# Kept weight units, an in-place residual and a split first tile between the output projection and the MLP

## The chip, the cores and the metric

The kernel runs as one program on one core of a Trainium2 chip. A core has a matrix engine (TensorE, PE in the profile, with its weight loads in a row of their own, PEld), a vector engine (VectorE, DVE), a scalar engine (ScalarE, ACT), GpSimd (POOL) and SyncE (SP), whose queue starts most of the transfers here. Each engine works through its own queue in order, and waits for the others by semaphores. The metric is the device time of the whole program in microseconds; smaller is better.

## The reference

One layer of a hybrid trunk for 384 tokens (256 of a prompt, 8 times 16 of running streams) of width 2048. The part that matters here is how the mixer's result becomes the input of the MLP:

```python
def rmsnorm(x, g):
    xf = x.astype(jnp.float32)
    y = xf * lax.rsqrt(jnp.mean(xf * xf, axis=-1, keepdims=True) + EPS)
    return (y * g.astype(jnp.float32)).astype(x.dtype)
...
    merged = (gates[:, :, 0] * br_pool + gates[:, :, 1] * br_ssd).astype(u.dtype)
    out = merged @ p['w_out']
...
    x = x + rmsnorm(m, p['g_mix_post'])
    hdn = jnp.square(jax.nn.relu(rmsnorm(x, p['g_mlp_pre']) @ p['w_up'])) @ p['w_down']
    x = x + rmsnorm(hdn, p['g_mlp_post'])
```

`w_out` is 2048 by 2048, `w_up` 2048 by 8192, `w_down` 8192 by 2048, all float32.

## The kernel before

The 384 tokens are three blocks of 128, called b = 0, 1, 2. Every large product is made with operands split into a high and a low part of type float32r, so that one product takes three matmuls: high by high, high by low, low by high (`mm3`, lines 80 to 83, and `mm` in `moving`, lines 644 to 646). The input that is split on the chip is split by two instructions: ACT copies it to the high part, DVE subtracts that from the original and writes the low part.

A weight unit is 128 by 1024 numbers, 512 KB. `wfetch` loads it into a tile `w`, `wsplit` writes its parts `wh` (ACT, line 72) and `wl` (DVE, line 74). Each of the three tiles has three buffers, so a unit's transfer waits until the unit three before it has been split, and a unit's split waits until PE has used the unit three before it for the last time.

The output projection is computed by `moving`: tokens are the stationary operand, the weights move, 512 columns at a time. There are four column groups (nb = 0 to 3) of eight units each, and three PSUM tiles `wo`, one for each block. For nb = 0 to 2 every unit is used for the three blocks at once. For nb = 3 the last three units are kept (`tail` = 3): they are used first for block 0, then for block 1, then for block 2, so that block 0 is complete earlier. After each block `done(b)` runs: ACT squares the result and sums it (line 692), for nb = 3 `postnorm` computes the root of the mean in a chain of small instructions on DVE and one on ACT (lines 663 to 674), and DVE multiplies the result with the norm's weight into the tile `hm` (line 695). When all three blocks are through, the residual is formed: `x1 = hm * y + x1` for each block and each 512 columns (line 707 on DVE; two of the twelve by line 704 on ACT and 705 on POOL). `x1` holds the input tokens until then; they are loaded by three transfers of 1 MB.

Next `x1` is transposed for the MLP: for each of 16 groups of 128 channels (k) PE transposes the three blocks into one PSUM tile `trm` (line 717), ACT writes the high part `x1h` (line 721) and DVE the low part `x1l` (line 722), 384 columns each. Four PSUM tiles `ss` serve these transposes and later the tile `bc`, so the transposes of group k wait until `x1l` of group k - 4 is written. The MLP's first product, tile `up0` (line 751 to 754), takes 48 matmuls of 384 columns over these 16 groups; `up1` and the others follow (line 756).

In the meantime the second norm is computed: ACT squares `x1` in twelve pieces (line 733), `postnorm` makes a factor for each token, DVE puts it on a diagonal (`dg`, line 737), and PE spreads it over the partitions with one float32 matmul with a matrix of ones (`bc`, line 739). ACT copies the result to `r2`, which the first evacuation of an up tile needs (line 759).

A scheduler of the language decides where in an engine's queue each instruction stands; the queue is then fixed. `issue_after` (in `wsplit`, through the variable `hold`) forces the split of the second half of `up0`'s weights and of those of `up1` behind the residual's instructions:

```python
        gate = [root[0], None]
...
            if i == 0:
                gate[1] = ins
...
                    hold[:] = gate
                    half(ps, 1, wload(io["w_up"][0, 1], "up0_1"), xs2)
```

Of the kernel before, what the change touches and what calls it, by code (L numbers as in the profile page):

```python
# [14 lines left out]
P = 128  # L15
T = 384
# [3 lines left out]
DM = 2048  # L20
KD = DM // P
# [13 lines left out]
def build(ctx, tc, io):  # L35
    nc = tc.nc
    v, s, te, gp, sy = nc.vector, nc.scalar, nc.tensor, nc.gpsimd, nc.sync
# [19 lines left out]
    hold = [None, None]  # L57

    def behind(ins):
        return nullcontext() if ins is None else tc.issue_after(ins.ins)  # L60

    def wfetch(src, name):
        w = wpool.tile([P, 1024], F32, tag="w", name=f"w_{name}")
        sy.dma_start(w, src)
        return w, name

    def wsplit(f):
        w, name = f
        h = wpool.tile([P, 1024], F32R, tag="wh", name=f"wh_{name}")
        l = wpool.tile([P, 1024], F32R, tag="wl", name=f"wl_{name}")  # L70
        with behind(hold[0]):
            s.activation(h, w, AF.Copy)  # L72
        with behind(hold[1]):
            v.tensor_tensor(l, w, h.bitcast(F32), ALU.subtract)  # L74
        return h, l

    def wload(src, name):
        return wsplit(wfetch(src, name))

    def mm3(out, wh, wl, xh, xl, first, last):  # L80
        te.matmul(out, wh, xh, start=first, stop=False)  # L81
        te.matmul(out, wh, xl, start=False, stop=False)  # L82
# [550 lines left out]

    x1 = res.tile([P, 3, DM], F32, name="x1")
    r2 = res.tile([P, T], F32, name="r2")

    def moving(o, units, lhs, tail, done):
        nk = len(lhs)

        def mm(b, wh, wl, k, k2):  # L640
            t = slice(b * P, b * P + P)
            c = slice(k2 * 512, k2 * 512 + 512)
            mh, ml = lhs[k][0][:, t], lhs[k][1][:, t]
            te.matmul(o[b], mh, wh[:, c], start=k == 0, stop=False)  # L644
            te.matmul(o[b], mh, wl[:, c], start=False, stop=False)  # L645
            te.matmul(o[b], ml, wh[:, c], start=False, stop=k == nk - 1)  # L646

        n = len(units)
        for kp in range(n - tail):
            wh, wl = wload(*units[kp])  # L650
            for k2 in range(2):
                for b in range(3):
                    mm(b, wh, wl, kp * 2 + k2, k2)
        w = [wload(*units[kp]) for kp in range(n - tail, n)]
        for b in range(3):
            for i, (wh, wl) in enumerate(w):
                for k2 in range(2):
                    mm(b, wh, wl, (n - tail + i) * 2 + k2, k2)
            done(b)

    root = [None]

    def postnorm(pool, st, b, name):
        pre, ms, rt, y = (pool.tile([P, 1], F32, tag=f"n{i}", name=f"n{i}_{name}{b}", bufs=3) for i in range(4))
        v.tensor_tensor(pre, st[:, b, 0:1], st[:, b, 1:2], ALU.add)
        v.tensor_tensor(pre, pre, st[:, b, 2:3], ALU.add)
        v.tensor_scalar(pre, pre, 1.0 / DM, EPS, ALU.mult, ALU.add)
        root[0] = s.activation(rt, st[:, b, 3:4], AF.Sqrt, bias=pre, scale=1.0 / DM)
# [4 lines left out]
        v.tensor_tensor(y, y, ms, ALU.mult)  # L673
        return y

    blk = lambda i: slice(i * 512, i * 512 + 512)
    for b in range(3):
        sy.dma_start(x1[:, b, :], io["x_tok"][b])
    with tc.tile_pool(name="phf", bufs=1, side="right", reuse_waits="tile") as pf, tc.tile_pool(
        name="phf2", bufs=2, side="right", reuse_waits="tile"  # L680
    ) as pf2:
        hm = pf.tile([P, 3, DM], F32, name="hm")
        st = pf.tile([P, 3, 4], F32, name="st1")
        ys = []
        for nb in range(4):
            gpo = pf2.tile([P, 512], F32, tag="gpo", name=f"gpo{nb}")
            sy.dma_start(gpo, io["g_mix_post"][blk(nb)].partition_broadcast(P))
            o = [mmtile(f"wo{nb}_{b}") for b in range(3)]

            def done(b):  # L690
                q = pf2.tile([P, 512], F32, tag="q", name=f"q1_{nb}_{b}")
                s.activation(q, o[b], AF.Square, accum_out=st[:, b, nb : nb + 1])
# [4 lines left out]
            moving(o, [(io["w_out"][nb, kp], f"wo{nb}_{kp}") for kp in range(8)], ms_, 3 if nb == 3 else 0, done)  # L697
        gate = [root[0], None]
        for i in range(4):
            for b in range(3):  # L700
                xb = x1[:, b, blk(i)]
                if b == 1 and i >= 2:
                    hb = hm[:, b, blk(i)]
                    s.activation(hb, hb, AF.Copy, scale=ys[b])
                    gp.tensor_tensor(xb, xb, hb, ALU.add)
                    continue
                ins = v.scalar_tensor_tensor(
                    out=xb, in0=hm[:, b, blk(i)], scalar=ys[b], in1=xb, op0=ALU.mult, op1=ALU.add
                )
            if i == 0:  # L710
                gate[1] = ins
    pga = ctx.enter_context(tc.tile_pool(name="pga", bufs=1, reuse_waits="tile"))
    xs2 = []
    for k in range(KD):
        tr = sstile(f"trm{k}")
        for b in range(3):
            te.transpose(tr[:, b * P : b * P + P], x1[:, b, k * P : k * P + P], ident)
        h = pga.tile([P, T], F32R, name=f"x1h{k}")
        l = pga.tile([P, T], F32R, name=f"x1l{k}")
        g1 = vec[:, V_GMLP + k : V_GMLP + k + 1]  # L720
        s.activation(h, tr[:, :T], AF.Copy, scale=g1)  # L721
        v.scalar_tensor_tensor(out=l, in0=tr[:, :T], scalar=g1, in1=h.bitcast(F32), op0=ALU.mult, op1=ALU.subtract)
        xs2.append((h, l))
    mpool.close()

    with tc.tile_pool(name="phg", bufs=1, reuse_waits="tile") as pg, tc.tile_pool(
# [3 lines left out]
        for b in range(3):  # L730
            for i in range(4):
                q = pg2.tile([P, 512], F32, tag="q3", name=f"q2_{b}_{i}")
                s.activation(q, x1[:, b, blk(i)], AF.Square, accum_out=st[:, b, i : i + 1])
        dg = pg.tile([P, 3, P], F32, name="dg2")
        for b in range(3):
            y = postnorm(pg2, st, b, "n2")
            v.tensor_scalar(dg[:, b, :], ident, y, None, ALU.mult)
        bc = sstile("bc2")
        te.matmul(bc[:, :T], ones, dg.rearrange("p b t -> p (b t)"), start=True, stop=True)
# [6 lines left out]
        for c8 in range(NC):  # L746
            hh = []
            for f8 in range(8):
                f = c8 * 8 + f8
                if f == 0:  # L750
                    ps = mmtile("pj_up0")[:, :T]
                    half(ps, 0, wload(io["w_up"][0, 0], "up0_0"), xs2)
                    hold[:] = gate
                    half(ps, 1, wload(io["w_up"][0, 1], "up0_1"), xs2)
                else:
                    ps = proj([io["w_up"][f, 0], io["w_up"][f, 1]], xs2, f"up{f}")
                    hold[:] = [None, None]
# [158 lines left out]
```

## Time and profile before

| What | Time |
|---|---|
| median of three runs | 2858.26 us (2857.53 to 2859.85) |
| the profiled execution, its time | 2857.06 us |
| the profiled execution, its span | 2855.3 us |
| PE busy | 99% of the span |
| DVE, ACT, POOL busy | 55%, 38%, 4% of the span |
| mean granted PE clock | 0.997 |

The span is the time from the first to the last recorded instruction; the execution's own time is 1.76 us more. A row of the timeline gives the start, the duration, the engine, the line of the source, the operation, what is written and read, the shape and how many like it were merged; in brackets stands how long the engine had been idle before it and who ended that. The durations of matmuls are modelled and overlap; the distance from one start to the next is what a matmul costs in a sequence.

### The profile page before, as it was taken

The page shows a single profiled execution, that of the slowest core. Times are in us where ns is not written, and L with a number is a line of the kernel's source. Part 1 is how long each engine was busy: PE and PEld are TensorE (multiplying, and loading weights), DVE is VectorE, ACT ScalarE, POOL GpSimd, SP SyncE. Part 2 cuts the span into 40 slices and gives each one's busy share as a digit, 9 for nine tenths or more (in the row PEclk, how much of TensorE's full clock was granted, in tenths as well). Part 3 has the DMA queues.
Part 4 walks back from the last instruction along what each step waited for, and adds up shares of the span by engine and source line. Part 5 has one row for each costly group of instructions (what it writes and reads, how often), then busy time and mean ns, then how long its engine had stood idle before and what let it go on. Part 6 is the DMA issues. An engine that isn't in the chain of part 4 may idle for free.

```text
span 2855.3 us, 39378 instructions
## 1 busy us (share of the span) xinstructions
PE 2830.0 (99%) x15855; PEld 2678.6 (94%) x15855; DVE 1568.3 (55%) x2231; ACT 1084.8 (38%) x1560; POOL 115.3 (4%) x163
## 2 busy tenths in 40 slices
PE   9999999999999999999999999999999999999998
PEld 8999999999999999999999987989899998989896
DVE  7674335678778778777533334524444444444445
ACT  5343224345345345444422234433233333323233
POOL 0000000001001001011000000000000000000001
PEclk9999999999999999999999999999999999999999
DMA  6444445466456566466644453344444344333343
GB/s 204 138 132 142 137 140 193 144 211 218 159 203 216 161 205 212 162 213 234 203 153 148 144 189 119 126 133 126 126 128 129 126 129 130 126 129 130 126 127 117
DMA packets 141656, 448.78 MB, mean 157 GB/s; under 512 B 17201, under 2 KB 40817, under 8 KB 136865
## 3 DMA queue, kind: packets, MB, share of 16 engines
q1 hardware_dynamic: 133152, 410.14, 44.7%
q0 software_dynamic: 8320, 36.13, 3.3%
q8 instruction: 124, 2.03, 0.3%
q14 instruction: 60, 0.48, 0.1%
HBM read 404.48 MB, written 41.72 MB: 156 GB/s over the span
## 4 chain that ended last, share of the span: by engine, by line
PE 95%; DVE 2%; ACT 1%; issue 1%; DMA 0%; SPq 0%; DVEq 0%; ACTq 0%
PE pj_up L82 6%; PE pj_up L83 6%; PE pj_up L81 6%; PE wd L645 6%; PE wd L646 6%; PE wd L644 6%; PE pj_x L83 5%; PE pj_x L81 5%; PE pj_x L82 5%; PE pj_sp L83 3%; PE pj_z L81 3%; PE pj_sp L82 3%; PE pj_z L82 3%; PE pj_sp L81 3%; PE pj_z L83 3%; PE pj_gb L81 2%
## 5 line engine op out<-in xcount | busy, mean ns | idle before, releaser
L82 PE MATMUL pj_up<-x1l,wh_up 128*128 128x384 f32 x1024 | 343.2, 335 | 0.0
L81 PE MATMUL pj_up<-x1h,wh_up 128*128 128x384 f32 x1024 | 343.0, 335 | 0.0
L83 PE MATMUL pj_up<-x1h,wl_up 128*128 128x384 f32 x1024 | 342.7, 335 | 0.0
L74 DVE TENSOR_TENSOR wl_wd<-w_wd,wh_wd 128x1024 fp32r<-128x1024 f32 x128 | 156.9, 1226 | 263.1 <-ACT wh_wd L72 263.1
L646 PE MATMUL wd<-wh_wd,hl 128*128 128x512 f32 x768 | 298.9, 389 | 0.0
L645 PE MATMUL wd<-wl_wd,hh 128*128 128x512 f32 x768 | 298.9, 389 | 0.0
L644 PE MATMUL wd<-wh_wd,hh 128*128 128x512 f32 x768 | 298.7, 389 | 0.0
L72 ACT ACTIVATE wh_wd<-w_wd 128x1024 fp32r<-128x1024 f32 x128 | 135.9, 1062 | 351.0 <-PE wd L646 284.4
L74 DVE TENSOR_TENSOR wl_up<-w_up,wh_up 128x1024 fp32r<-128x1024 f32 x128 | 156.9, 1226 | 198.0 <-ACT wh_up L72 198.0
L72 ACT ACTIVATE wh_up<-w_up 128x1024 fp32r<-128x1024 f32 x128 | 135.8, 1062 | 325.8 <-PE pj_up L82 265.1
L81 PE MATMUL pj_x<-xgh,wh_x 128*128 128x384 f32 x768 | 258.2, 336 | 0.0
L82 PE MATMUL pj_x<-xgl,wh_x 128*128 128x384 f32 x768 | 257.8, 336 | 0.0
L83 PE MATMUL pj_x<-xgh,wl_x 128*128 128x384 f32 x768 | 257.7, 336 | 0.0
L81 PEld LDWEIGHTS pj_up<-x1h,wh_up 128*128 128x128 f32 x1024 | 192.5, 188 | 0.7 <-ACT x1h L721 0.4
L82 PEld LDWEIGHTS pj_up<-x1l,wh_up 128*128 128x128 f32 x1024 | 192.6, 188 | 0.4
L83 PEld LDWEIGHTS pj_up<-x1h,wl_up 128*128 128x128 f32 x1024 | 192.4, 188 | 0.1
L644 PEld LDWEIGHTS wd<-wh_wd,hh 128*128 128x128 f32 x768 | 144.2, 188 | 29.9
L646 PEld LDWEIGHTS wd<-wh_wd,hl 128*128 128x128 f32 x768 | 144.1, 188 | 29.9
L645 PEld LDWEIGHTS wd<-wl_wd,hh 128*128 128x128 f32 x768 | 144.1, 188 | 29.8
L83 PE MATMUL pj_z<-xgh,wl_z 128*128 128x384 f32 x512 | 171.0, 334 | 0.0
L81 PE MATMUL pj_z<-xgh,wh_z 128*128 128x384 f32 x512 | 171.0, 334 | 0.0
L82 PE MATMUL pj_z<-xgl,wh_z 128*128 128x384 f32 x512 | 171.0, 334 | 0.0
(279 smaller groups left out, 6145.6 us busy)
## 6 DMA issues: line engine op xcount, KB each, us to landing
w_up<-w_up SPq DMA_DIRECT2D x128, 512.0 KB, 3.4
w_wd<-w_down SPq DMA_DIRECT2D x128, 512.0 KB, 3.4
w_x<-w_in SPq DMA_DIRECT2D x96, 512.0 KB, 4.3
w_z<-w_in SPq DMA_DIRECT2D x64, 512.0 KB, 4.4
w_sp<-w_ssd SPq DMA_DIRECT2D x64, 512.0 KB, 3.5
w_ga<-w_in SPq DMA_DIRECT2D x32, 512.0 KB, 3.4
w_pp<-w_pp SPq DMA_DIRECT2D x32, 512.0 KB, 3.4
hs<-ssm SPq DMA_DIRECT2D x16, 1024.0 KB, 5.6
```

What stands on the lines that cost most here:

```text
L72: s.activation(h, w, AF.Copy)
L74: v.tensor_tensor(l, w, h.bitcast(F32), ALU.subtract)
L81: te.matmul(out, wh, xh, start=first, stop=False)
L82: te.matmul(out, wh, xl, start=False, stop=False)
L83: return te.matmul(out, wl, xh, start=False, stop=last)
L644: te.matmul(o[b], mh, wh[:, c], start=k == 0, stop=False)
L645: te.matmul(o[b], mh, wl[:, c], start=False, stop=False)
L646: te.matmul(o[b], ml, wh[:, c], start=False, stop=k == nk - 1)
```

## The change

Between the output projection and the up projection four things are different.

1. For nb = 3 five units are kept instead of three. The split parts of the first three live in the usual buffers; those of the last two have tiles of their own (`eh`, `el`). Each block thus has 30 matmuls in a row instead of 18.
2. `hm` is gone. `x1` takes the product of the projection and the norm's weight, and the residual is formed in place right after each block's root: `x1 = x1 * y + xt`. The input tokens come in twelve tiles `xt` of 256 KB with six buffers. All twelve residual instructions are on DVE; the two on ACT and the two on POOL are gone, as is the forced order (`hold`, `gate`).
3. The transposes are made for blocks 0 and 1 first (256 columns in one PSUM tile), then for block 2 (128 columns). Tile `up0` is computed in two parts as well: 48 matmuls of 256 columns over blocks 0 and 1, then 48 of 128 columns for block 2. Its two weight units stay until both parts are done.
4. The diagonal of the second norm is split into a high and a low part, and `bc` is made by two float32r matmuls instead of one float32 matmul.

```diff
-        with behind(hold[0]):
-            s.activation(h, w, AF.Copy)
-        with behind(hold[1]):
-            v.tensor_tensor(l, w, h.bitcast(F32), ALU.subtract)
+        s.activation(h, w, AF.Copy)
+        v.tensor_tensor(l, w, h.bitcast(F32), ALU.subtract)
...
-        w = [wload(*units[kp]) for kp in range(n - tail, n)]
+        w = [wload(*units[kp]) for kp in range(n - tail, n - max(0, tail - 3))]
+        for kp in range(n - max(0, tail - 3), n):
+            f, name = wfetch(*units[kp])
+            h = pool.tile([P, 1024], F32R, name=f"eh_{name}")
+            l = pool.tile([P, 1024], F32R, name=f"el_{name}")
+            s.activation(h, f, AF.Copy)
+            v.tensor_tensor(l, f, h.bitcast(F32), ALU.subtract)
+            w.append((h, l))
...
-    for b in range(3):
-        sy.dma_start(x1[:, b, :], io["x_tok"][b])
...
+            if nb == 3:
+                for b in range(3):
+                    for i in range(4):
+                        xt[b, i] = pf2.tile([P, 512], F32, tag="xt", name=f"xt{b}_{i}", bufs=6)
+                        sy.dma_start(xt[b, i], io["x_tok"][b][:, blk(i)])
...
                 s.activation(q, o[b], AF.Square, accum_out=st[:, b, nb : nb + 1])
+                v.tensor_tensor(x1[:, b, blk(nb)], o[b], gpo, ALU.mult)
                 if nb == 3:
-                    ys.append(postnorm(pf2, st, b, "n1"))
-                v.tensor_tensor(hm[:, b, blk(nb)], o[b], gpo, ALU.mult)
...
-        gate = [root[0], None]
-        for i in range(4):
-            for b in range(3):
-                xb = x1[:, b, blk(i)]
-                if b == 1 and i >= 2:
-                    hb = hm[:, b, blk(i)]
-                    s.activation(hb, hb, AF.Copy, scale=ys[b])
-                    gp.tensor_tensor(xb, xb, hb, ALU.add)
-                    continue
-                ins = v.scalar_tensor_tensor(
-                    out=xb, in0=hm[:, b, blk(i)], scalar=ys[b], in1=xb, op0=ALU.mult, op1=ALU.add
-                )
+                    y = postnorm(pf2, st, b, "n1")
+                    for i in range(4):
+                        xb = x1[:, b, blk(i)]
+                        v.scalar_tensor_tensor(out=xb, in0=xb, scalar=y, in1=xt[b, i], op0=ALU.mult, op1=ALU.add)
+            moving(
+                o, [(io["w_out"][nb, kp], f"wo{nb}_{kp}") for kp in range(8)], ms_, 5 if nb == 3 else 0, done, pf
+            )
...
+    def turn(k, b0, b1):
+        tr = sstile(f"trm{k}_{b0}")
+        n = (b1 - b0) * P
+        for b in range(b0, b1):
+            te.transpose(tr[:, (b - b0) * P : (b - b0 + 1) * P], x1[:, b, k * P : k * P + P], ident)
+        h, l = (x[:, b0 * P : b1 * P] for x in xs2[k])
+        g1 = vec[:, V_GMLP + k : V_GMLP + k + 1]
+        s.activation(h, tr[:, :n], AF.Copy, scale=g1)
+        v.scalar_tensor_tensor(out=l, in0=tr[:, :n], scalar=g1, in1=h.bitcast(F32), op0=ALU.mult, op1=ALU.subtract)
+
+    w0 = [wload(io["w_up"][0, q], f"up0_{q}") for q in range(2)]
+    up0 = mmtile("pj_up0")[:, :T]
+
+    def up_first(b0, b1):
+        t = slice(b0 * P, b1 * P)
+        for k in range(KD):
+            h, l = w0[k // 8]
+            c = slice(k % 8 * P, k % 8 * P + P)
+            mm3(up0[:, t], h[:, c], l[:, c], xs2[k][0][:, t], xs2[k][1][:, t], k == 0, k == KD - 1)
+
     for k in range(KD):
-        tr = sstile(f"trm{k}")
...
+        turn(k, 0, 2)
+    up_first(0, 2)
+    for k in range(KD):
+        turn(k, 2, 3)
+    up_first(2, 3)
...
-        dg = pg.tile([P, 3, P], F32, name="dg2")
+        dg = pg.tile([P, 2, 3, P], F32R, name="dg2")
         for b in range(3):
             y = postnorm(pg2, st, b, "n2")
-            v.tensor_scalar(dg[:, b, :], ident, y, None, ALU.mult)
+            v.tensor_scalar(dg[:, 0, b], ident, y, None, ALU.mult)
+            v.scalar_tensor_tensor(
+                out=dg[:, 1, b], in0=ident, scalar=y, in1=dg[:, 0, b].bitcast(F32), op0=ALU.mult, op1=ALU.subtract
+            )
         bc = sstile("bc2")
-        te.matmul(bc[:, :T], ones, dg.rearrange("p b t -> p (b t)"), start=True, stop=True)
+        for i in range(2):
+            te.matmul(bc[:, :T], onesr, dg[:, i].rearrange("p b t -> p (b t)"), start=i == 0, stop=i == 1)
```

More of the change, by code (lines that the diff above doesn't have):

```diff
@@ L635, in build, with moving @@
     r2 = res.tile([P, T], F32, name="r2")
-    def moving(o, units, lhs, tail, done):
+    blk = lambda i: slice(i * 512, i * 512 + 512)
+    def moving(o, units, lhs, tail, done, pool=None):
         nk = len(lhs)
@@ L659, in moving @@
             done(b)
-    root = [None]
     def postnorm(pool, st, b, name):
@@ L676, in build @@
     blk = lambda i: slice(i * 512, i * 512 + 512)
-    for b in range(3):
-        sy.dma_start(x1[:, b, :], io["x_tok"][b])
+    pga = ctx.enter_context(tc.tile_pool(name="pga", bufs=1, reuse_waits="tile"))
     with tc.tile_pool(name="phf", bufs=1, side="right", reuse_waits="tile") as pf, tc.tile_pool(
@@ L681, in build @@
     ) as pf2:
-        hm = pf.tile([P, 3, DM], F32, name="hm")
         st = pf.tile([P, 3, 4], F32, name="st1")
-        ys = []
+        xt = {}
         for nb in range(4):
@@ L692, in done @@
                 s.activation(q, o[b], AF.Square, accum_out=st[:, b, nb : nb + 1])
+                v.tensor_tensor(x1[:, b, blk(nb)], o[b], gpo, ALU.mult)
                 if nb == 3:
-                    ys.append(postnorm(pf2, st, b, "n1"))
-                v.tensor_tensor(hm[:, b, blk(nb)], o[b], gpo, ALU.mult)
-            moving(o, [(io["w_out"][nb, kp], f"wo{nb}_{kp}") for kp in range(8)], ms_, 3 if nb == 3 else 0, done)
-        gate = [root[0], None]
-        for i in range(4):
-            for b in range(3):
-                xb = x1[:, b, blk(i)]
-                if b == 1 and i >= 2:
-                    hb = hm[:, b, blk(i)]
-                    s.activation(hb, hb, AF.Copy, scale=ys[b])
-                    gp.tensor_tensor(xb, xb, hb, ALU.add)
-                    continue
-                ins = v.scalar_tensor_tensor(
-                    out=xb, in0=hm[:, b, blk(i)], scalar=ys[b], in1=xb, op0=ALU.mult, op1=ALU.add
-                )
-            if i == 0:
-                gate[1] = ins
@@ L712, in build @@
-    pga = ctx.enter_context(tc.tile_pool(name="pga", bufs=1, reuse_waits="tile"))
-    xs2 = []
-    for k in range(KD):
-        tr = sstile(f"trm{k}")
[L716 to L723, printed above, removed]
+                    y = postnorm(pf2, st, b, "n1")
@@ new lines, in done @@
+                    for i in range(4):
[4 more added lines that the diff above has]
+            )
+    xs2 = [
+        (pga.tile([P, T], F32R, name=f"x1h{k}"), pga.tile([P, T], F32R, name=f"x1l{k}")) for k in range(KD)
+    ]
+    def turn(k, b0, b1):
[7 more added lines that the diff above has]
+        v.scalar_tensor_tensor(out=l, in0=tr[:, :n], scalar=g1, in1=h.bitcast(F32), op0=ALU.mult, op1=ALU.subtract)
@@ L750, in build @@
                 if f == 0:
[L751 to L754, printed above, removed]
+                    ps = up0
                 else:
                     ps = proj([io["w_up"][f, 0], io["w_up"][f, 1]], xs2, f"up{f}")
-                    hold[:] = [None, None]
                 t = pg2.tile([P, T], F32, tag="t", name=f"ht{f}")
```

3 lines of the change are left out of this document (1 added, 2 removed).

## The prediction

> **What bounds the kernel now.** I read the page first, then the matmuls of the stage in order of time, then the same stretch by windows, and last what ACT and DVE did in it.
>
> ```profile
> span 2855.3 us, 39378 instructions
> PE 2830.0 (99%) x15855; PEld 2678.6 (94%) x15855; DVE 1568.3 (55%) x2231; ACT 1084.8 (38%) x1560; POOL 115.3 (4%) x163
> ```
>
> PE sets the time, so only places where PE waits or runs slowly can give anything. The stage in question is one:
>
> ```profile
> 1772.01 0.39 PE L646 MATMUL wo<-wh_wo,ml 128*128 128x512 f32 x1
> 1773.31 0.66 PE L717 MATMUL trm<-cst,x 128*128 128x128 f32 x4 [0.47 <-DVE x L707]
> 1777.17 1.12 PE L717 MATMUL trm<-cst,x 128*128 128x128 f32 x4 [3.21 <-DVE x L707]
> 1793.60 0.33 PE L82 MATMUL pj_up<-x1l,wh_up 128*128 128x384 f32 x1
> 1798.49 0.88 PE L739 MATMUL bc<-dg,cst 128*128 128x384 f32 x2
> 1799.56 0.34 PE L81 MATMUL pj_up<-x1h,wh_up 128*128 128x384 f32 x1
> 1802.68 0.33 PE L81 MATMUL pj_up<-x1h,wh_up 128*128 128x384 f32 x1
> ...
> 1772.20:1776.60 4.40, 1.29 (x9) 0.77 (x7) 4.22 (x11) 3.99 (x7) 2.48 (x2) 0.98 0.42 121
> 1776.60:1783.40 6.80, 5.84 (x23) 4.68 (x23) 5.84 (x10) 4.81 (x12) 0.56 (x1) 0.51 0.37 145
> 1783.40:1793.70 10.30, 10.30 (x70) 10.10 (x69) 8.98 (x23) 10.30 (x31) 0.00 (x0) 1.00 0.23 66
> ```
>
> The projection ends at 1772.24, `up0` at 1793.60, tile `up2` begins at 1802.68; after that PE runs without a gap, so the start of `up2` is my mark. PE waits 3.2 us for block 2's residual, and for 6.8 us it has half its clock (0.51; the columns behind the five engines are granted clock, DMA share and GB/s). In the third window ACT is busy all the time: it feeds the transposes' high parts and the second norm's squares. From 1772.24 to 1802.68 are 30.44 us. At the steps worked out below, 96 matmuls of 384 columns (16.6), 48 transposes (4.0), a dozen changes between the two (1.0) and `bc` (0.9) are 22.5 us; the other 7.9 are waits and half clock, and no change here can give more than these.
>
> **The change part by part.** *Kept units.* The same matmuls run in another order: no PE time. Units 6 and 7 have tiles of their own; only unit 5's split waits for a buffer, as here:
>
> ```profile
> 1752.04 1.06 ACT L72 ACTIVATE wh_wo<-w_wo 128x1024 fp32r<-128x1024 f32 x1 [3.02 <-PE wo L646]
> 1753.13 1.23 DVE L74 TENSOR_TENSOR wl_wo<-w_wo,wh_wo 128x1024 fp32r<-128x1024 f32 x1 [2.85 <-ACT wh_wo L72]
> w_up<-w_up SPq DMA_DIRECT2D x128, 512.0 KB, 3.4
> ```
>
> The tail of 90 matmuls (0.227 us from start to start) now begins at 1751.8; unit 5 is ready at 1754.36 and needed 12 matmuls in, at 1754.6: just in time. Unit 7's buffer is free at about 1750.3 and its split done 3.4 + 1.06 + 1.23 us later, 1756.1, needed at 1757.3. Cost 0, and the lateness itself if a transfer is late. Block 0's result then comes at 1758.6, block 1's at 1765.4, so their residuals end near 1765 and 1770 under block 1's and 2's matmuls. The two waits for `x1` of 0.5 and 3.2 us are gone. On SP's queue six `xt` transfers now stand ahead of `up1`'s second unit and wait for DVE's residuals; they are issued by 1769, and that unit is needed after 1794. Cost 0.
>
> *In front of block 2's residual.* In the changed queue of DVE three weight splits (`up0` twice, `up1` once) stand ahead of block 2's product; the forced order that held two of them back is gone. They start when block 1's residuals are done, about 1770.05.
>
> ```profile
> 1774.44 1.99 ACT L72 ACTIVATE wh_up<-w_up 128x1024 fp32r<-128x1024 f32 x2
> 1790.84 1.22 DVE L74 TENSOR_TENSOR wl_up<-w_up,wh_up 128x1024 fp32r<-128x1024 f32 x1
> 1772.44 0.60 ACT L692 ACTIVATE q<-wo 128x512 f32<-128x512 f32 x1 [1.66 <-PE wo L646]
> 1776.37 2.74 DVE L707 SCALAR_TENSOR_TENSOR x<-hm,n_n,x 128x512 f32<-128x512 f32 x4
> 1775.24 1.09 DVE L673 TENSOR_TENSOR n_n<-n_n,n_n 128x1 f32<-128x1 f32 x1
> 1777.68 2.00 ACT L721 ACTIVATE x1h<-trm,vec 128x384 fp32r<-128x384 f32 x4 [1.26 <-PE trm L717]
> 1779.02 2.18 DVE L722 SCALAR_TENSOR_TENSOR x1l<-trm,vec,x1h 128x384 fp32r<-128x384 f32 x4
> ```
>
> A merged row of n gives the step from one to the next: (2.74 - 0.75) / 3 = 0.665 for a residual of 512 columns, (2.18 - 0.61) / 3 = 0.52 for `x1l` of 384, hence 0.39 for 256 and 0.26 for 128; likewise on ACT 0.47 for `x1h`, 0.93 for 1024 columns, hence 0.37 for 256 and 0.28 for 128. A weight split steps by 1.14. The three splits end at 1773.47, block 2's product at 1774.13, and the first `x1l` at 1774.8. (The 1.09 us of one 1-column instruction while POOL ran its two additions goes away with them; it lay in the wait of 3.2 us.)
>
> *First part of `up0`.* The work is 32 transposes, 48 matmuls of 256 columns, and a penalty where a matmul follows transposes:
>
> ```profile
> 566.26 1.12 PE L581 MATMUL su<-xst,bst 128*128 128x256 f32 x8
> 1786.00 0.49 PE L717 MATMUL trm<-cst,x 128*128 128x128 f32 x3
> 1786.25 0.42 PE L81 MATMUL pj_up<-x1h,wh_up 128*128 128x384 f32 x1
> 1786.51 0.49 PE L717 MATMUL trm<-cst,x 128*128 128x128 f32 x3
> 1792.04 0.33 PE L81 MATMUL pj_up<-x1h,wh_up 128*128 128x384 f32 x1
> 1792.21 0.33 PE L82 MATMUL pj_up<-x1l,wh_up 128*128 128x384 f32 x1
> ```
>
> Three transposes take 0.25 (0.083 each), a matmul behind them 0.26 instead of 0.173, so 0.087 a change; a float32r matmul of 256 columns (1.12 - 0.28) / 7 = 0.12. Sum 2.7 + 5.8 + 13 x 0.087 = 9.6 us. The waits: 0.7 for the first `x1h` (behind block 2's square on ACT, so 1772.44 + 0.6 + 0.5 against 1772.9, when the four groups that have buffers are transposed), 1.1 for the first `x1l` (it frees the transposes' buffer), and then block 2's four residuals: in DVE's queue they stand between `x1l` of groups 3 and 4, 1776.3 to 1778.9, and PE, which needs `x1l` of group 4 to go on, stops from 1777.3 to 1779.45, 2.1 us. Together 3.9; the part ends at 1772.24 + 9.6 + 3.9 = 1785.7.
>
> *Second part.* Four transposes and a first `x1h` of 128 columns: PE goes on at 1786.7 and is through the first matmul and one of `up1` by 1787.1. Left are 12 transposes (1.0), 12 changes (1.04) and 47 matmuls of 128 columns. No row of this trace has float32r at 128 columns. The nearest rows:
>
> ```profile
> 551.82 1.06 PE L542 MATMUL pp<-Bk,xdw 128*128 128x128 f32 x8
> L542 PE MATMUL pp<-Bk,xdw 128*128 128x128 f32 x128 | 16.9, 275 | 0.0
> L581 PE MATMUL su<-xst,bst 128*128 128x256 f32 x128 | 17.9, 282 | 0.0
> ```
>
> Low end: 0.12 for 256 columns and 0.173 for 384 on a line give 0.067 for 128. High end: the plain float32 product of just this shape, two records of (1.06 - 0.275) / 7 = 0.112, so 0.224. I take 0.224, the row that has the shape; the split into two parts pays three loads of the same weights either way, and one third of the columns. Then `up0` ends at 1787.1 + 2.04 + 47 x 0.224 = 1799.7. In a sentence apart: the Trainium skill, "TensorE: Matmul & The Clock Gate", section on the back-to-back issue gap, gives about 81 ns for each pair of weight load and matmul at 128 columns; by it this part would end at 1793.0, 6.7 us earlier (no run shows it yet; the transposes' 0.083 agrees). That would not gain 6.7 us, for the reason that follows.
>
> *`bc` and what is queued behind it.* In the changed PE queue `bc` stands directly behind `up0`, and 47 of the 48 matmuls of `up1` stand behind `bc`. In the old queue `bc` came 28 matmuls later, under which the second norm was hidden. When is `bc`'s input ready?
>
> ```profile
> 1791.83 0.66 ACT L733 ACTIVATE q<-x 128x512 f32<-128x512 f32 x1
> 1792.44 0.66 ACT L733 ACTIVATE q<-x 128x512 f32<-128x512 f32 x1
> 1793.67 0.68 ACT L668 ACTIVATE n_n<-st,n_n 128x1 f32<-128x1 f32 x3
> L737 DVE TENSOR_SCALAR dg<-cst,n_n 128x128 f32<-128x128 f32 x3 | 0.8, 281 | 0.0
> ```
>
> From 1786.25 ACT makes 16 `x1h` (16 x 0.28 = 4.5), five squares (5 x 0.61 = 3.1) and the wait for one transposed group (0.2), to 1794.1; three roots to 1794.5; the split of `up1`'s second unit to 1795.5. On DVE its low part, behind block 0's diagonal, takes 1796.1 to 1797.3, and four diagonal instructions (0.2 apart) end at 1798.15. So `bc` can't begin before 1798.2. With 0.224 a matmul PE gets there later, at 1799.8, and waits for nothing; below 0.19 the norm decides. `bc` as two float32r matmuls costs 0.35 against some 0.9, then 47 x 0.1733 = 8.15 us.
>
> **The sum.** `up2` begins at 1799.8 + 0.35 + 8.15 = 1808.3 or, with half a dozen handovers of some 0.03, 1808.5. That is 5.8 us after 1802.68. Profiled execution: 2857.06 + 5.8 = 2862.9. It lies 1.2 below the median of the runs; the difference is added to the median: 2858.26 + 5.8 = 2864.1. With the low end: 1798.2 + 0.35 + 8.15 = 1806.7, or +4.0.
>
> **The rivals.** *The narrow matmul is cheap* (0.19 or less). For it speaks the line through 256 and 384; against it that everything non-transposed at 128 columns costs 0.22. PE then waits up to 4.4 us for the norm: 2858.26 + 4.0 = 2862.3. Chance 0.30.
>
> *Half clock again.* Before, the clock fell at 1776.60 after 3.4 us with nothing but eight transposes. Now PE has from 1772.24 to 1779.45 only 13 matmuls and 16 transposes, about 3.3 us of work in 7.2. If that is too little, the work between, say, 1776.6 and 1783.4 doubles: some of it falls into waits, the rest adds 0.9 to 2.8 us: 2858.26 + 5.8 + 1.9 = 2866.0. Against it: no stop is as long as the 3.2 us of before. Chance 0.27. In a sentence apart: the same page of the Trainium skill, section on the PE-mode transpose, says that transposes don't count as PE activity, which speaks for this rival; its section on the clock gate puts the idle window at about 3.4 us, which agrees with the trace.
>
> *Not slower.* If ACT never waits from 1772.44 on, its work up to the last diagonal is 0.6 + 16 x 0.37 + 0.2 + 12 x 0.61 + 16 x 0.28 + 0.6 + 0.93 = 20.1 us, DVE's rest 1.14 + 0.8, and `bc` begins at 1794.5. With cheap narrow matmuls `up2` then starts at 1803.0: +0.3, 2858.6. It needs the 2.1 us stop behind block 2's residual and the first waits to vanish, which DVE's queue does not allow. It decides if `x1l` is never the last to come. Chance 0.07. A true gain would need `bc` to be waited for elsewhere.
>
> **How the numbers follow.** Forecast 0.36, cheap 0.30, half clock 0.27, not slower 0.07. The range goes from the cheap case with ACT and DVE 1.2 us quicker (2861.0) to half clock at its full price less the handovers and a little (2867.2). A measurement of this kernel tells about 0.2%, 5.7 us, from no change, and my forecast of 5.8 lies on that line: its chance is halved, of half clock 0.25 is beyond, of cheap 0.08 (with half clock as well): slower 0.52, within 0.44, faster 0.04.
>
> **What would show it.** Right: the two waits on `x1` gone; a stop of 2 us in the middle of the first part, ended by `x1l` of group 4; 128-column matmuls 0.22 apart; `bc` right behind `up0`, and `up2` 36 us after the projection. Cheap: 128-column matmuls 0.07 to 0.19 apart and a wait of 1 to 4 us for `dg`. Half clock: PEclk near 0.5 in a stretch of 3.4 or 6.8 us. Wrong altogether: `up2` less than 30 us after the projection, or a stop in the kept units.

## The result, and the profile after

The changed kernel takes 2864.18 us (median of 20 runs, 2860.87 to 2867.15), the kernel before 2857.84 us (median of 20, 2856.04 to 2859.85): ratio 1.0022, 95% interval 1.0016 to 1.0028. It is slower, by some 6 us or 0.2%, close to the time that was forecast. The trace shows that terms of the forecast's sum were wrong and cancelled, so that the number came out by luck. The profiled execution of the changed kernel took 2863.16 us.

The page of the changed kernel, span and busy time of each engine:

```profile
span 2861.3 us, 39530 instructions
PE 2833.6 (99%) x15903; PEld 2682.9 (94%) x15903; DVE 1571.4 (55%) x2252; ACT 1086.0 (38%) x1574; POOL 113.1 (4%) x161
```

The timeline of PE in the changed kernel, from the projection's last matmul to the first of `up2` (start, duration, what; in brackets the idle time in front and what ended it):

```profile
1772.65 0.39 PE L643 MATMUL wo<-eh_wo,ml 128*128 128x512 f32 x1
...
1774.19 0.38 PE L77 MATMUL pj_up<-x1h,wh_up 128*128 128x256 f32 x1 [0.27 <-ACT x1h L719]
1775.98 0.44 PE L716 MATMUL trm<-cst,x 128*128 128x128 f32 x2 [1.41 <-DVE x1l L720]
...
1780.51 0.44 PE L716 MATMUL trm<-cst,x 128*128 128x128 f32 x2 [0.44 <-DVE x1l L720]
...
1786.51 0.60 PE L716 MATMUL trm<-cst,x 128*128 128x128 f32 x4
1787.67 0.55 PE L77 MATMUL pj_up<-x1h,wh_up 128*128 128x128 f32 x2 [0.56 <-ACT x1h L719]
...
1794.49 0.28 PE L77 MATMUL pj_up<-x1h,wh_up 128*128 128x128 f32 x1
...
1796.06 0.27 PE L79 MATMUL pj_up<-x1h,wl_up 128*128 128x128 f32 x1
1798.30 0.97 PE L757 MATMUL bc<-dg,onesr 128*128 128x384 f32 x2 [1.97 <-DVE dg L751]
1799.10 0.34 PE L78 MATMUL pj_up<-x1l,wh_up 128*128 128x384 f32 x1
...
1808.82 0.33 PE L77 MATMUL pj_up<-x1h,wh_up 128*128 128x384 f32 x1
```

The projection ends 0.23 us, one step, after its last start: 1772.88. From there to `up2` are 35.94 us; before it was 30.44. The difference, 5.5 us, is nearly the whole difference of the two profiled executions (2863.16 - 2857.06 = 6.1; the other 0.64 us lie ahead of the stage). The two waits for `x` are gone. In their place stand two stops for `x1l` (1.41 and 0.44 us), small ones between the narrow matmuls, and 1.97 us in front of `bc`. The narrow matmuls of 128 columns follow one another in (1796.06 - 1794.49) / 14 = 0.112 us, half the price taken.

The same stretch by windows (length, busy time of PE, PEld, DVE, ACT, POOL with instructions, then granted clock, DMA share, GB/s):

```profile
1772.80:1776.60 3.80, 2.12 (x15) 1.60 (x13) 3.80 (x10) 2.47 (x8) 0.54 (x1) 0.96 0.78 252
1776.60:1780.00 3.40, 3.40 (x18) 3.27 (x16) 3.40 (x8) 1.83 (x5) 0.00 (x0) 0.54 0.98 377
1780.00:1786.50 6.50, 6.06 (x52) 5.99 (x52) 5.52 (x17) 6.50 (x19) 0.00 (x0) 1.00 0.15 60
1786.50:1796.20 9.70, 8.40 (x67) 7.58 (x65) 7.12 (x35) 9.65 (x34) 0.00 (x0) 1.00 0.01 2
1796.20:1800.10 3.90, 1.85 (x10) 1.47 (x9) 3.90 (x12) 1.54 (x2) 0.00 (x0) 1.00 0.26 72
1800.10:1803.60 3.50, 3.50 (x13) 3.50 (x12) 0.83 (x2) 1.05 (x2) 0.00 (x0) 0.51 0.60 219
1803.60:1809.00 5.40, 5.40 (x33) 5.40 (x32) 1.22 (x1) 1.21 (x2) 0.00 (x0) 1.00 0.16 39
```

Half clock comes twice, each time for 3.4 us (the first time from 1776.3 on, a little ahead of the window shown), and each time behind a window in which PE stood for part of the time. The 47 matmuls of `up1` behind `bc` take 1808.82 - 1799.10 = 9.72 us in place of 8.15: the second half clock costs 1.57 us there. The whole stage as one window, first of the kernel before, then of the changed one:

```profile
1772.20:1802.70 30.50, 26.38 (x148) 23.95 (x147) 25.86 (x64) 24.23 (x56) 3.04 (x3) 0.89 0.41 134
```

```profile
1772.90:1808.80 35.90, 30.43 (x195) 28.58 (x194) 25.69 (x79) 24.10 (x68) 0.54 (x1) 0.90 0.31 107
```

This pair is the shortest account of the loss. PE stood 4.1 us before (30.50 - 26.38) and stands 5.5 us now; it was busy 26.4 us and is busy 30.4. The granted clock is the same, 0.89 and 0.90. So the waits did not go, they moved and grew by 1.4 us, and PE got 4 us more of busy time. Half clock falls on 6.8 us of that time now and fell on 5.8 before; without what it adds to each (about half of that), the work grew by some 3.5 us, from 23.5 to 27.0. What `bc` waits for is seen on DVE in the changed kernel:

```profile
1771.26 3.49 DVE L70 TENSOR_TENSOR wl_up<-w_up,wh_up 128x1024 fp32r<-128x1024 f32 x3
1774.67 0.68 DVE L698 TENSOR_TENSOR x<-wo,gpo 128x512 f32<-128x512 f32 x1
...
1777.33 2.73 DVE L703 SCALAR_TENSOR_TENSOR x<-x,n_n,xt 128x512 f32<-128x512 f32 x4
1779.98 3.38 DVE L720 SCALAR_TENSOR_TENSOR x1l<-trm,vec,x1h 128x256 fp32r<-128x256 f32 x8
...
1796.64 1.22 DVE L70 TENSOR_TENSOR wl_up<-w_up,wh_up 128x1024 fp32r<-128x1024 f32 x1
1797.77 0.47 DVE L751 TENSOR_SCALAR dg<-cst,n_n 128x128 fp32r<-128x128 f32 x2
1798.16 0.61 DVE L752 SCALAR_TENSOR_TENSOR dg<-cst,n_n,dg 128x128 fp32r<-128x128 f32 x2
```

Three weight splits ahead of block 2's product, four residuals ahead of the fifth `x1l`, and a weight split between the diagonals: the queue stands as it was read from the order of the instructions.

### The profile page after: what moved, and what is told of

The parts are those of the page before. It is cut to its first block, busy times and chain, and to the rows that moved or that the text cites. A ratio compares the mean times of both kernels' runs of the same rounds, so it can differ in the third digit from the quotient of the medians.

```text
span 2861.3 us, 39530 instructions
## 1 busy us (share of the span) xinstructions
PE 2833.6 (99%) x15903; PEld 2682.9 (94%) x15903; DVE 1571.4 (55%) x2252; ACT 1086.0 (38%) x1574; POOL 113.1 (4%) x161
## 3 DMA queue, kind: packets, MB, share of 16 engines
q8 instruction: 124, 2.03, 0.3%
## 4 chain that ended last, share of the span: by engine, by line
PE 95%; DVE 2%; ACT 1%; issue 1%; DMA 0%; SPq 0%; DVEq 0%; ACTq 0%
PE pj_up L77 6%; PE pj_up L78 6%; PE pj_up L79 6%; PE wd L642 6%; PE wd L643 6%; PE wd L641 6%; PE pj_x L79 5%; PE pj_x L77 5%; PE pj_x L78 5%; PE pj_sp L79 3%; PE pj_z L77 3%; PE pj_z L78 3%; PE pj_sp L78 3%; PE pj_sp L77 3%; PE pj_z L79 3%; PE pj_gb L77 2%
## 5 line engine op out<-in xcount | busy, mean ns | idle before, releaser
L77 PE MATMUL pj_up<-x1h,wh_up 128*128 128x384 f32 (+1 forms) x1040 | 347.2, 334 | 0.8 <-ACT x1h L719 0.8
L78 PE MATMUL pj_up<-x1l,wh_up 128*128 128x384 f32 (+2 forms) x1040 | 347.6, 334 | 0.0
L79 PE MATMUL pj_up<-x1h,wl_up 128*128 128x384 f32 (+2 forms) x1040 | 347.1, 334 | 0.0
```

## The experiments

Three theories were set against each other. A: `bc` in front of its input, the wait that this brings, and the work that two parts add, are the loss. B: the three weight splits ahead of block 2's product are. C: half clock comes whatever PE does, and is the loss. "Stage" is always the time from the projection's end to `up2`, in the one profiled run of each kernel (two for the kernel with two splits back). Medians are of 11 runs each, beside 21 to 33 runs of the kernel before on the same chip (medians 2857.97 to 2858.04 us); the first two rows are of 20 runs each.

| kernel | stage, us | median, us | ratio to before (95%) |
|---|---|---|---|
| before | 30.44 | 2857.84 | |
| changed | 35.94 | 2864.18 | 1.0022 (1.0016 to 1.0028) |
| `bc` late | 33.12 | 2860.38 | 1.0009 (1.0 to 1.0018) |
| two splits back | 39.4, 33.91 | 2860.97 | 1.0013 (1.0005 to 1.0022) |
| one pass | 30.49 | 2856.74 | 0.9995 (0.9986 to 1.0003) |
| filler ahead of `bc` | 34.38 | 2862.43 | 1.0017 (1.0008 to 1.0026) |
| `bc` late, two splits back | 32.77 | 2860.91 | 1.0012 (1.0003 to 1.002) |
| one pass, two splits back | 28.20 | 2856.14 | 0.9995 (0.9986 to 1.0004) |
| one pass, tail of three | 32.82 | 2860.07 | 1.0007 (0.9998 to 1.0016) |
| + last residual back | 28.5 | 2855.73 | 0.9994 (0.9985 to 1.0003) |
| + filler | 27.42 | 2855.51 | 0.9992 (0.9983 to 1.0001) |

**`bc` behind half of `up1`.**

```diff
         bc = sstile("bc2")
-        for i in range(2):
-            te.matmul(bc[:, :T], onesr, ...)
+        up1 = mmtile("pj_up1")[:, :T]
+        half(up1, 0, wload(io["w_up"][1, 0], "up1_0"), xs2)
+        with behind(last[0]):
+            for i in range(2):
+                te.matmul(bc[:, :T], onesr, ...)
...
+        half(up1, 1, wload(io["w_up"][1, 1], "up1_1"), xs2)
```

> `bc` is emitted behind the first half of `up1` (24 matmuls) in place of directly behind `up0`; all else as in the changed kernel. The stage runs from the end of the projection's last matmul to the first matmul of `up2`: 30.44 us before, 35.94 us changed. Theory A (the loss is `bc` in front of its input, and what the wait brings with it): the wait of 2.0 us for `dg` is gone, the half clock at 1800.15 is gone too, because PE no longer stands in the 3.4 us ahead of it; behind the end of `up0` come 48 x 0.173 + 0.35 = 8.7 us, so the stage is 32.0 us, 3.9 us shorter, and the time some 3.9 us below the changed kernel (+1.6 over before). Theory B (the three weight splits ahead of block 2's product on DVE make the stage late): the norm's chain sets the end wherever `bc` stands, the gain is below 1 us. Theory C (the second half clock comes whatever PE does): only the wait goes, 2.0 us.

The timeline of PE, and the windows of this kernel:

```profile
1780.55 0.44 PE L716 MATMUL trm<-cst,x 128*128 128x128 f32 x2 [2.00 <-DVE x1l L720]
...
1801.52 0.50 PE L760 MATMUL bc<-dg,onesr 128*128 128x384 f32 x2
...
1806.04 0.33 PE L77 MATMUL pj_up<-x1h,wh_up 128*128 128x384 f32 x1
```

```profile
1772.90:1782.00 9.10, 5.42 (x43) 4.76 (x42) 9.10 (x22) 6.41 (x18) 0.54 (x1) 1.00 0.78 267
1782.00:1785.20 3.20, 3.20 (x18) 3.20 (x17) 2.62 (x8) 2.56 (x7) 0.00 (x0) 0.50 0.15 61
1785.20:1806.00 20.80, 19.86 (x139) 19.04 (x139) 14.29 (x51) 15.50 (x45) 0.00 (x0) 1.00 0.20 61
```

No idle time stands in front of `bc`, and the second half clock is gone, as theory A wanted. The median fell by 3.8 us (3.9 expected). The stage of the profiled run fell by 2.8 only, and the reason can be seen in the same rows. Here the half clock begins at 1782.0, behind the stop for block 2's residuals, and all that it adds to the work is lost. In the changed kernel it began at 1776.3, ahead of that stop: the work grew into the stop, which shrank from 2.00 to 0.44 us. Both kernels have the same instructions up to there, and yet the half clock begins 3.4 us behind the projection's end in one profile and 9.1 us in the other.

**Two weight splits back.** The low part of `up0`'s second unit and of `up1`'s first are issued after block 2's last residual:

```diff
-        v.tensor_tensor(l, w, h.bitcast(F32), ALU.subtract)
+        with behind(after):
+            v.tensor_tensor(l, w, h.bitcast(F32), ALU.subtract)
...
-    w0 = [wload(io["w_up"][0, q], f"up0_{q}") for q in range(2)]
+    w0 = [wload(io["w_up"][0, q], f"up0_{q}", resid[0] if q else None) for q in range(2)]
```

> Two of the three low parts of weights (second unit of `up0`, first of `up1`) are held back on DVE until block 2's last residual; all else as in the changed kernel. Block 2's product, its residuals and the first `x1l` come 2 x 1.14 = 2.3 us earlier. Theory A: that shortens the stops of PE in the first part (1.41 and 0.44 us behind `x1l`), `up0` ends 1 to 2 us earlier, but `bc` then waits longer for the same `dg`, which hangs on ACT's work; the stage gains 0 to 1.2 us (34.7 to 35.9). Theory B: all 2.3 us or more go through to the end: 33.6 us or less.

> The kernel with the two low parts held back once more, for a second profile: the first fell on the slowest of its eleven runs (2866.7, median 2861.0), with five windows of half clock in the stage. If the spread is the number of such windows, a run near the median has one or two, and its stage is about 6 us shorter than in the first profile (39.5 us), 33 to 34 us.

Median 2860.97, 3.2 us below the changed kernel, so more than theory A allowed (0 to 1.2 us). By size alone the run is nearer to B, which asked for a stage of 33.6 us or less and sees 33.91. The rows show where the gain comes from. The second profile, of a run at 2860.40, on PE:

```profile
1780.03 0.44 PE L720 MATMUL trm<-cst,x 128*128 128x128 f32 x2 [3.13 <-DVE x1l L724]
...
1797.46 0.57 PE L761 MATMUL bc<-dg,onesr 128*128 128x384 f32 x2
...
1806.03 0.33 PE L78 MATMUL pj_up<-x1h,wh_up 128*128 128x384 f32 x1
```

```profile
1796.40 0.47 DVE L755 TENSOR_SCALAR dg<-cst,n_n 128x128 fp32r<-128x128 f32 x2
```

The projection ended at 1772.12 here, so `bc` begins 25.34 us behind it; in the changed kernel it was 25.42. The diagonal's high parts are complete 24.75 us behind it (1796.87), in the changed kernel 25.36: the earlier splits brought the norm's chain 0.6 us, not 2.3, and `bc` 0.1. PE comes to `bc` half a microsecond after its input, since the 2.00 us stop in the first part has grown to 3.13 (a split and four residuals stand together there) and the half clock falls behind it, on work. So PE doesn't stand in front of `bc`, and no half clock follows. From `bc` to `up2` are 8.57 us in place of 10.52, and that is nearly all of the 2.03 us by which the stage is shorter. A was right on where the chain is and wrong on the price of standing still; an earlier residual that goes through to the end, as B has it, is not what these rows show.

**One pass over all three blocks.** The first two parts of the change stay, the split of the transposes and of `up0` goes:

```diff
     for k in range(KD):
-        turn(k, 0, 2)
-    up_first(0, 2)
-    for k in range(KD):
-        turn(k, 2, 3)
-    up_first(2, 3)
+        turn(k, 0, 3)
+    up_first(0, 3)
```

> The kept units, the residual in place and the splits ahead of block 2's product stay; the transposes and `up0` go over all three token blocks at once (384 columns), as before the change, and `bc` falls into `up1` again. Theory A: the first complete group waits for block 2's first residual, some 4.2 us behind the projection's end; from there to `up2` the kernel before needs 1802.68 - 1777.17 = 25.5 us, so the stage is about 29.7 us (29 to 31), 5 to 6.5 us shorter than in the changed kernel, and the time equal to before within 1 us. Theory B: the splits are still there, so at least 2.3 us of the loss stay: 32.5 us or more.

On PE, and the window of half clock:

```profile
1777.26 0.66 PE L716 MATMUL trm<-cst,x 128*128 128x128 f32 x4 [3.16 <-DVE x L703]
...
1798.79 0.41 PE L754 MATMUL bc<-dg,onesr 128*128 128x384 f32 x1
...
1803.55 0.33 PE L77 MATMUL pj_up<-x1h,wh_up 128*128 128x384 f32 x1
```

```profile
1778.70:1785.60 6.90, 6.00 (x25) 5.42 (x25) 5.13 (x10) 5.26 (x13) 0.00 (x0) 0.51 0.46 178
```

The old picture is back whole: a wait of 3.2 us for `x`, 6.9 us of half clock, `bc` inside `up1`, and the stage of before to 0.05 us. The splits still stand ahead of block 2's product, and yet 5.5 us are gone: theory B falls. The split into two parts, with the place of `bc` that follows from it, is the whole loss, 2864.2 against 2856.7 us. What `bc` as two float32r matmuls gives by itself wasn't run.

**Filler ahead of `bc`.** Eighteen matmuls on constants, whose result is overwritten, go into the wait for `dg`:

```diff
         bc = sstile("bc2")
+        with behind(last[0]):
+            for i in range(18):
+                te.matmul(bc[:, :P], onesr, onesr, start=True, stop=True)
```

> 18 matmuls of 128 columns in float32r on constants, whose result is thrown away (`bc` overwrites it), stand between the end of `up0` and `bc`; they need 18 x 0.111 = 2.0 us and fill the wait for `dg`. If the half clock at 1800.15 follows from PE standing in the 3.4 us before it: it is gone, and the stage is 1.5 us shorter, 34.4 us. If the half clock comes for another reason (theory C): no change, 35.9 us or 0.1 to 0.3 more. If the narrow matmul costs 0.224 rather than 0.111, `bc` is 2.0 us later.

On PE, and the window behind it:

```profile
1795.63 2.17 PE L758 MATMUL bc<-onesr 128*128 128x128 f32 x18
1797.77 0.97 PE L760 MATMUL bc<-dg,onesr 128*128 128x384 f32 x2
...
1806.73 0.33 PE L77 MATMUL pj_up<-x1h,wh_up 128*128 128x384 f32 x1
```

```profile
1799.90:1803.30 3.40, 3.40 (x22) 3.40 (x21) 0.56 (x1) 1.74 (x3) 0.00 (x0) 1.00 0.63 193
```

More work on PE made the kernel quicker: `bc` begins where it did (25.42 us behind the projection's end, 1772.35 here), the clock stays at 1.00, and the stage is 34.38, 1.56 shorter. The profiled run is the quickest of its eleven (2861.03 us), but the median agrees: 2862.43, 1.75 us below the changed kernel. Theory C falls, since the half clock does depend on what PE does before it: in no profile in which PE runs into `bc` at full clock without a stop does half clock follow it. Eighteen matmuls with a step of (2.17 - 0.28) / 17 = 0.111 us also measure the narrow matmul by itself.

**Both edits on the split kernel.** `bc` late and two splits back together:

> Both edits at once: `bc` behind the first half of `up1`, and the two low parts of weights held back on DVE until block 2's last residual. `bc` late took the median from 2864.2 to 2860.4, the two splits alone to 2861.0. Theory A (the three-part view: the wait behind `bc`, the work that the split into two parts adds, half clock): the two gains overlap, since both shorten the same wait for `dg`; what the splits add on top is the earlier first `x1l`, at most the 1.4 us stop in the first part. 2859 to 2860.4, still 1 us or more above before. Theory B (DVE's order and `bc` together are all of the loss): 3.8 + 3.2 us go, 2857.2, not slower than before.

The whole stage as one window, and the longest stop on PE:

```profile
1775.60:1808.40 32.80, 27.27 (x196) 25.58 (x195) 25.85 (x79) 24.24 (x68) 0.54 (x1) 1.00 0.38 122
```

```profile
1783.52 0.44 PE L720 MATMUL trm<-cst,x 128*128 128x128 f32 x2 [3.13 <-DVE x1l L724]
```

The profiled run has no half clock at all and no wait for `dg`, and the stage is still 32.8 us. The two gains don't add up (2860.9, within A's span but for half a microsecond). What remains is work, 27.3 us of it, and a stop of 3.13 us behind block 2's residuals. (This run, at 2862.73 us, is above its kernel's median; its projection ended 2.7 us later than in the changed kernel, at 1775.61, ahead of all edits.)

**One pass, tail of three.**

> As the kernel with transposes and `up0` over all three blocks (2856.7 us), but with a tail of three kept units as before the change: only the residual in place per block remains of the change. Block 0's and block 1's results then come 18 x 0.227 = 4.1 us apart, and a block takes DVE a product (0.68), a norm chain (1.0) and four residuals (2.7), 4.4 us, plus the splits between them. If five kept units do what the prediction said (they take the residuals of blocks 0 and 1 under PE's work): block 2's first residual comes 1 to 3 us later, the stage is 31.5 to 33.5 us and the time 2857.7 to 2859.7. If they are worth nothing: 2856.7.

```profile
1775.18 0.71 PE L716 MATMUL trm<-cst,x 128*128 128x128 f32 x4 [2.20 <-DVE x L703]
1779.72 1.11 PE L716 MATMUL trm<-cst,x 128*128 128x128 f32 x4 [3.83 <-DVE x L703]
```

```profile
1775.70:1785.90 10.20, 5.98 (x24) 4.69 (x23) 9.60 (x19) 4.75 (x11) 0.54 (x1) 0.50 0.67 241
```

The timeline of PE has its two waits for `x` again, 2.20 and 3.83 us, half clock lasts 10.2 us in place of the 6.9 of the kernel with five, and the median is 2860.07, a little above the span expected. So the five kept units are worth 3.3 us (2860.07 - 2856.74), the half clock that they save included. The residual in place with a tail of three is some 2 us worse than before, where POOL and ACT took two of the residuals; the interval of that ratio, 0.9998 to 1.0016, just includes no loss, and what makes the difference wasn't tried.

**Toward a better version.** Three kernels go on from the one pass, each with one edit more. First, of the three splits only the first stays ahead of block 2's product:

```diff
+    w0 = [wload(io["w_up"][0, 0], "up0_0")]
...
+        ins = turn(k, 0, 3)
+        if k == 3:
+            w0.append(wload(io["w_up"][0, 1], "up0_1", ins))
```

> As the kernel with transposes and `up0` over all three blocks (2856.7 us), but of the three weight splits ahead of block 2's product on DVE only the first stays there: that of `up0`'s second unit goes behind `x1l` of group 3, that of `up1`'s first unit behind block 2's last residual. Block 2's first residual then hangs on the square and the root on ACT: the root ended at 1774.3, the chain of 1-column instructions needs 1 us, so it starts at 1775.6 in place of 1776.45, and PE's wait of 3.16 us for it shrinks to 2.3. Theory A: 0.9 us less, 2855.8 (2855 to 2856.3), and some 1.7 us more in runs where the shorter stop saves a window of half clock. Theory B: 2.3 us less, 2854.4.

Then block 2's fourth residual stands on DVE behind the fifth `x1l` instead of ahead of the first:

```diff
+                    for i in range(4 if b < 2 else 1):
+                        residual(i)
...
+            if k in (1, 2, 5):
+                resid[1]({1: 1, 2: 2, 5: 3}[k])
+            ins = turn(k, 0, 3)
```

> As the kernel with one pass over all three blocks and two splits moved back (2856.1 us, stage 28.2 us with one window of half clock); in addition block 2's fourth residual stands behind `x1l` of groups 0 to 4 on DVE, not ahead of group 0. The first `x1l` comes 0.66 us earlier, and PE's stop of 0.90 us in front of it shrinks to some 0.25: 2855.5, if the stop is on the path. If the stop only moves (`x1l` of group 5 now waits for the residual and a weight split, 1.8 us, with 1.6 us of PE work ahead of it): no gain, 2856.1.

And ten matmuls on constants stand in PE's wait for block 2's first residual:

```diff
+            if k == 3 and b == 1:
+                with behind(tp):
+                    for i in range(10):
+                        te.matmul(up0[:, :P], onesr, onesr, start=True, stop=True)
```

> As the kernel just before it, and ten matmuls of 128 columns on constants (1.1 us; the result is thrown away) in PE's stop of 2.3 us ahead of block 2's first residual. If PE's idle time in a window of 3.4 us brings the half clock, windows with half clock become rarer: 1 to 1.7 us less in most runs, about 2854.3, and a granted clock of 0.998 in place of 0.997. If ten matmuls are too few to hold the clock: 2855.5 and no change of the clock; they can't cost anything, since PE waits there longer than they last.

On PE of the first of the three, then the filler of the last, and the whole stage of the last as one window:

```profile
1775.39 0.66 PE L720 MATMUL trm<-cst,x 128*128 128x128 f32 x4 [2.30 <-DVE x L705]
```

```profile
1773.22 1.31 PE L731 MATMUL pj_up<-onesr 128*128 128x128 f32 x10
```

```profile
1772.40:1799.90 27.50, 25.06 (x157) 22.75 (x156) 23.53 (x63) 21.30 (x52) 0.54 (x1) 1.00 0.38 119
```

The wait for `x` shrank from 3.16 to 2.30 us, to the number expected, and the median by 0.6 (0.9 expected). (The stages of the first and the last in the table, 28.20 and 27.42, are those of the quickest of eleven runs; in the last two kernels one matmul of `up1`, 0.17 us, stands behind the first of `up2`, outside the stage.) The fourth residual gave 0.4 and the filler 0.2 more; neither step can be told from none by its median. With the filler the profiled run has no half clock (2854.29 us), and five of its eleven runs lie between 2854.3 and 2854.8 us; without it one of eleven did. The other six lie where the kernel without filler does, so ten matmuls may hold the clock in some runs and not in all. The last kernel's median, 2855.51, is 2.5 us below that of before, with an interval that ends at 1.0001: probably a little faster, not shown to be.

The two windows without half clock, this one and that of both edits on the split kernel, give the price of the split directly. In two parts PE is busy 27.27 us; in one pass 25.06. The filler adds 1.07 to that, as its 1.31 us overlap the transposes ahead by 0.24, and some 0.1 of the last matmul of `up1` lies outside: 24.1 without the filler. The split costs 3.2 us of PE work here, and some 3.5 by the pair of windows at the start.

## Why the prediction was right, and where it was wrong

The stage, by the prediction's own steps:

| step | forecast, us | measured, us |
|---|---|---|
| projection's end to end of the first part | 13.46 | 13.63 |
| second part | 14.0 | 9.66 |
| from there to `bc` | 0.1 | 2.13 |
| `bc` to `up2` | 8.7 | 10.52 |
| sum | 36.26 | 35.94 |

(Measured: 1772.88, 1786.51, then 1796.06 and a step of 0.11, 1798.30, 1808.82.)

*Kept units at nothing: right.* PE is busy without a gap up to the projection's end. Beyond the prediction, the tail of five is worth 3.3 us where the transposes wait for all blocks; the split kernel wasn't run with a tail of three.

*The first part: right in sum, by another way.* The wait for the first `x1l` was 1.41 us, not 1.1. The stop of 2.1 us behind the four residuals is there with 2.00 us where the clock is full (`bc` late), and 0.44 us where half clock falls on it. Half clock made PE's work longer by about what it took from the stop. The argument against half clock, that no stop is as long as the 3.2 us of before, didn't hold: it came behind stops of 0.27 and 1.41 us.

*The second part: the step that failed.* "I take 0.224, the row that has the shape" took the price of plain float32 for float32r. Measured is 0.111 at 128 columns, in both the kernel and the filler. The line through 256 and 384 columns (0.067) was too low as well: at 256 columns the step is 0.12, so from 256 down to 128 columns hardly anything is saved. The shape was the wrong thing to go by; the row to go by was the 256-column float32r matmul, with a weight load in front of each. In a sentence apart: the Trainium skill, "TensorE: Matmul & The Clock Gate", section on the back-to-back issue gap, has about 81 ns for such a pair, nearer than the forecast and still 30 ns below this trace.

*`bc`'s input: right.* It was put 25.96 us behind the projection's end, and `bc` began 25.42 behind it. With the cheap matmul the condition of the first rival holds, and PE waits 1.97 us for `dg`, inside its bounds of 1 to 4.

*Half clock: left out of the sum, and there.* It came twice, and the second time it followed from the very wait that the cheap matmul exposes; the filler showed this. The forecast's case gave it no price, and its rival placed it in the first part only.

So the time was met by two of the rivals together: cheap matmul, +4.0, and 1.57 us of half clock behind `bc`, 5.6 in all, where the stage shows 5.5. The failed price made the second part 4.3 us too long; a wait of 2 us, a `bc` of two records that took 0.8 us in place of 0.35 (the second waits for the last low part of `dg`, which ends at 1798.77), and the half clock filled that up. That these nearly cancelled is luck. What the forecast had right is the structure: `bc` and nearly all of `up1` stand behind `up0`, the second norm sets `bc`, and no narrow matmul however cheap could bring more than the norm allows. That the medians lie 6.3 us apart and the stages 5.5 agrees with the profiled run being one of the quicker ones of the changed kernel; where its windows of half clock fall is not the same in each run. (One sum of the forecast is off by a little: 0.18, 0.25 and 0.08 make a chance of 0.51 for slower, not 0.52.)

## What to carry to other kernels

A stage that is split so that its first part may start early pays for each part's weights again: count the matmuls at their price per instruction, not per column. Before moving work to fill a wait, list what stood under the work that is moved: here 28 matmuls of `up1` had hidden a norm. And weigh a split by windows of busy and idle time: it took the wait of 3.2 us for `x` away, put 3.2 to 3.5 us of work in, and the idle time came back in other places.

## What the runs showed of the hardware

- float32r matmuls with a weight load each step by 0.111 us at 128 columns, 0.120 at 256, 0.173 at 384 and 0.227 at 512: from 256 down to 128 the number of columns hardly counts.
- Half clock came in stretches of 3.4 us, of 6.8 and 6.9 (before, one pass) and of 10.2 (tail of three), mostly behind stops of PE of 1.4 to 3.2 us. It went away when the stop was filled with useless matmuls (34.38 against 35.94 us of stage). Its place moves from run to run: in the two profiles with two splits back it begins 9.2 and 8.2 us behind the projection's end. The length agrees with the 3.4 us that the Trainium skill's page named above gives in its section on the clock gate. Not every such stop brings it: the run with both edits had one of 3.13 us and no half clock. How much idle time in a window decides is open.
- Once half clock lasted 13.7 us, four times the usual length. It is the first profile with two splits back, here by windows and by PE's stops ahead of it:

```profile
1792.40:1806.10 13.70, 13.70 (x61) 13.54 (x61) 8.44 (x32) 6.70 (x17) 0.00 (x0) 0.50 0.15 55
```

```profile
1789.63 0.56 PE L78 MATMUL pj_up<-x1h,wh_up 128*128 128x128 f32 x2 [0.55 <-ACT x1h L723]
...
1792.07 0.33 PE L720 MATMUL trm<-cst,x 128*128 128x128 f32 x1 [0.36 <-DVE x1l L724]
```

PE was busy all the time and had narrow matmuls for most of it; the stops ahead were no longer than in the changed kernel, where no half clock followed at this place. That run took 2866.71 us. Why the clock stayed down wasn't tried.
